# Handing out the input projection of a two-layer trunk in half pieces

## The chip, the cores and the metric

The kernel runs on 1 core of a Trainium2 chip. The metric is the device time of one execution in microseconds (us). Engine names are those of the profile: PE is TensorE's matmul, PEld its weight load, DVE is VectorE, ACT is ScalarE, POOL is GpSimd, SP is SyncE, which issues the DMAs. A "granted clock" of 1.00 is 2.4 GHz and 0.50 is 1.2 GHz; a figure between them is a mean over a stretch.

## What is computed

Two layers over 512 tokens (256 of context, 256 latent) of width 1024. A layer normalises, multiplies by one input projection, gives its columns to four mixers that scan the tokens in both directions, joins the four outputs, multiplies by an output projection and adds the result to the stream. Then comes a feed-forward block, dense in the first layer and a mixture of 8 experts in the second. Cut to the parts that matter here:

```python
def layer(x):
    h = modulated_rms_norm(x)
    p = h @ w_in                      # 28 tiles of 128 columns
    y = concat(rglru(p), rwkv7(p), mlstm(p), gdn(p))
    x = x + gate * (y @ w_out)
    return x + gate2 * ffn(modulated_rms_norm(x))
```

## The kernel before, in words

Every matrix is split in two parts of fp32r, a high and a low one, and a product is three matmuls: high by high, low activation by high weight, high activation by low weight (`mm3`). A weight tile comes by DMA (`wsplit`, L251, issued at L257), ACT casts the high part (`whi`, L258) and DVE subtracts for the low part (`wlo`, L259). In an order or a profile a matmul `pj<-hh,whi` or `pj<-hl,whi` or `pj<-hh,wlo` is one of those three: of the input projection first, of the output projection later.

The mixer stage of a layer is written by `mixers` (L1494). It is a loop that hands out work by turns. In a turn the projection gives one **piece**: `inproj` (L415) yields after the 12 matmuls of one k for the first four column tiles, and after 4 of the 8 k, 12 matmuls too, for the 24 other tiles. Then the **filling** may move (the modulation blocks of later work, `mod_block`, whose weights `mw` come from `mod_w`), and then each of three **lanes** may move by some steps. A lane is a queue of mixer units; a step is what a unit does up to its next `yield`. How far each may go in a turn is a credit, which grows by the numbers of the table `PACE`: three for the lanes, one for the filling, chosen by the count of turns `n`. After the last piece the turns go on until the lanes are empty.

When the projection is through and only one mixer is left, the **early sums** begin: `outproj_part` (L1692) sums the output projection over the finished mixers' rows, for one of 8 column tiles m at a time: 6 of the 8 k, 18 matmuls. It loads the old stream (`pst`, L1700), adds (`resid`, L1718) and writes the sum to DRAM (`xo`, L1703). The loop takes one of its nine steps in every turn (L1640). The last mixer is the mLSTM (`mlstm`, L1290): its end is a chain over DVE, ACT and PE (L1393 to L1424), and its output is split into `hh` and `hl` (L1286, L1287). Then `outproj` (L1706) loads the early sums back (`xT<-xo`, L2032) and adds the last 2 k of each column tile, 6 matmuls each, 48 in all: the **final sums**. The first layer works on 512 columns there, the second on the 256 latent ones.

What stands in each engine's queue is fixed when the program is built. It follows the order in which the code is written, with small shifts: a few matmuls of a piece may stand ahead of a lane's step and the others behind it.

Of the kernel before, what the change touches and what calls it, by code (L numbers as in the profile page):

```python
# [180 lines left out]
class Trunk:  # L181
# [233 lines left out]
    def inproj(self, l, tiles, evac, lat_only=()):  # L415
        if sorted(tiles[0:4]) == list(range(4)):
            pss = [self.pjt() for _ in range(2)] + [self.ps(), self.ps()]
            for k in range(8):
                wh, wl = self.wsplit(self.t["w_in0"][l, :, k], 4, P)
                for i in range(4):  # L420
                    tl, lo = tiles[i], 256 if i in lat_only else 0
                    self.mm3(pss[i][:, lo:512], wh[:, tl], wl[:, tl], self.hh[:, k, lo:512], self.hl[:, k, lo:512],
                             k == 0, k == 7)
                if k < 7:
                    yield
            for i in range(4):
                evac(i, pss[i])
            yield
        for i, tl in enumerate(tiles):
            if tl < 4:  # L430
                continue
            ps = self.pjt()
            lo = 256 if i in lat_only else 0
            for k in range(8):
                if k % 4 == 0:
                    wh, wl = self.wsplit(self.t["w_in"][l, tl - 4, :, k:k + 4], 4, P)
                self.mm3(ps[:, lo:512], wh[:, k % 4], wl[:, k % 4], self.hh[:, k, lo:512], self.hl[:, k, lo:512],
                         k == 0, k == 7)
                if k % self.PIECE[l] == self.PIECE[l] - 1 and k < 7:
                    yield  # L440
            evac(i, ps)
            yield
# [1051 lines left out]
    def mixers(self, l, xsrc, xdst):  # L1494
# [129 lines left out]
        while self.going or filling or any(self.lanes):  # L1624
            if self.going:
                self.ph(f"inp{l}")
                self.going = next(pr, "end") != "end"
            pace = next((p for e, p in self.PACE[l] if n < e), self.PACE[l][-1][1])
            n += 1
            credit[3] += pace[3]  # L1630
            while filling and credit[3] >= 1:
                self.ph(f"modx{l}")
                filling = next(md, "end") != "end"
                credit[3] -= 1
            if part is None and not self.going and len(self.fill[l]) < full - 1 and len(self.left) <= self.PART[l]:
                self.early = [k for i, m in enumerate(("lru", "rwkv", "gdn", "mlstm")) if m not in self.left for k in (2 * i, 2 * i + 1)]
                part = self.outproj_part(l, self.early, xsrc, xdst)
            if part is not None:
                self.ph(f"outp{l}")
                next(part, None)  # L1640
            for i, q in enumerate(self.lanes):
                credit[i] = min(credit[i], 0) if not q else credit[i] + pace[i]
                while credit[i] >= 1:
                    credit[i] -= 1
                    while q:
                        self.ph(self.lab.get(id(q[0]), "mix"))
                        r = next(q[0], "end")
                        if r != "end":
                            self.lab[id(q[0])] = r
                            break  # L1650
                        q.pop(0)
# [2 lines left out]
        return [k for k in range(8) if k not in self.early]  # L1654

    PART = [1, 1]
    PIECE = [4, 4]
    NPP = (3, 2, 2)
    LANE = dict(gates=1, rwkv=0, gdn=1, mlstm=2, lru=2)
    LATE = (0, 2)  # L1660
# [537 lines left out]
```

## Time and profile before

| what | value |
|---|---|
| median of 3 runs | 1906.63 us (1901.4 to 1910.62) |
| the profiled execution | 1907.89 us |
| its span, first to last instruction | 1906.1 us |
| PE busy | 1726.9 us (91%) |
| PEld busy | 1428.8 us (75%) |
| DVE busy | 1233.9 us (65%) |
| ACT busy | 1009.4 us (53%) |
| mean granted clock | 0.923 |

Durations below come from the profiled execution, so a sum is made against its 1907.89 us. It lies 1.3 us above the median. Busy time on PE overlaps itself: a matmul of 512 columns is shown as 0.39 us long while the next one starts 0.23 us later. So starts are compared, or a count is divided into a stretch.

### The profile page before, as it was taken

The numbers are of one execution on the slowest core, as the hardware profiler recorded it, in microseconds if no ns is written. First come the engines' busy times: TensorE is split into PE (matmuls) and PEld (weight loads), VectorE is DVE, ScalarE is ACT, GpSimd is POOL, SyncE is SP. The second block draws the span as 40 slices with busy tenths as digits, with TensorE's granted clock in tenths as the row PEclk, the third lists the DMA queues.
The fourth block names the chain that finished last, engine by engine and source line by source line (L and its number), as shares of the span: only waits on it lengthen the run. The fifth ranks groups of instructions, "written<-read, shape, count | busy, mean of one in ns | idle before, by whom it ended". The sixth has DMA issues, their size and how long they took to land. (4 is left out here: it accounts for less than half of the span.)

```text
span 1906.1 us, 34059 instructions
## 1 busy us (share of the span) xinstructions
PE 1726.9 (91%) x13291; PEld 1428.8 (75%) x13291; DVE 1233.9 (65%) x2527; ACT 1009.4 (53%) x1760; POOL 33.5 (2%) x88
## 2 busy tenths in 40 slices
PE   4989988997987999999979898998886999999996
PEld 2767666774765888888867665776775999999995
DVE  4577368777656433333366747797655888888886
ACT  4554465774534333332255453677435776777673
POOL 0000001000000000000000000000000000000000
PEclk8969898998998999999988898999687999999998
DMA  7433333244452333333334444411264998989891
GB/s 278 145 105 124 121 128 112 66 136 152 140 178 67 97 98 99 95 97 94 97 131 138 134 142 144 137 62 49 69 197 147 350 347 298 354 286 356 314 342 74
DMA packets 130921, 309.71 MB, mean 162 GB/s; under 512 B 14208, under 2 KB 40064, under 8 KB 130624
## 3 DMA queue, kind: packets, MB, share of 16 engines
q1 hardware_dynamic: 130752, 307.46, 47.8%
q8 instruction: 106, 1.74, 0.4%
q14 instruction: 63, 0.52, 0.1%
HBM read 286.76 MB, written 20.64 MB: 161 GB/s over the span
## 5 line engine op out<-in xcount | busy, mean ns | idle before, releaser
L259 DVE TENSOR_TENSOR wlo<-w,whi 128x512 fp32r<-128x512 f32 (+2 forms) x488 | 501.0, 1033 | 327.0 <-ACT whi L258 311.6
L258 ACT CAST whi<-w 128x512 fp32r<-128x512 f32 (+2 forms) x488 | 436.7, 898 | 413.2 <-PE pj L244 145.4
L244 PE MATMUL pj<-hh,whi 128*128 128x512 f32 (+1 forms) x544 | 225.3, 415 | 32.1 <-ACT whi L258 15.7
L244 PE MATMUL pj<-hh,wlo 128*128 128x512 f32 (+1 forms) x544 | 220.7, 407 | 5.4 <-DVE wlo L259 5.2
L244 PE MATMUL pj<-hl,whi 128*128 128x512 f32 (+1 forms) x544 | 215.9, 397 | 0.4 <-DVE hl L1287 0.2
L244 PE MATMUL pm<-whi,xgh 128*128 128x384 f32 (+1 forms) x512 | 168.2, 329 | 0.0
L244 PE MATMUL pm<-whi,xgl 128*128 128x384 f32 (+1 forms) x512 | 166.6, 325 | 0.0
L244 PE MATMUL pm<-wlo,xgh 128*128 128x384 f32 (+1 forms) x512 | 166.1, 324 | 0.0
L244 PEld LDWEIGHTS pj<-hh,whi 128*128 128x128 f32 x544 | 114.1, 210 | 61.2 <-ACT whi L258 20.8
L244 PE MATMUL pj<-mw,sc 128*32 128x256 f32 x768 | 107.0, 433 | 53.1 <-DMA mw<-in_mod_w 52.9
L244 PEld LDWEIGHTS pj<-hh,wlo 128*128 128x128 f32 x544 | 113.2, 208 | 35.1 <-DVE wlo L259 11.2
L244 PEld LDWEIGHTS pj<-hl,whi 128*128 128x128 f32 x544 | 114.1, 210 | 17.7 <-DVE hl L1287 0.9
L244 PE MATMUL pd<-whi,hth 128*128 128x256 f32 x352 | 100.1, 285 | 0.3
L244 PE MATMUL pd<-wlo,hth 128*128 128x256 f32 x352 | 99.2, 282 | 0.0
L244 PEld LDWEIGHTS pj<-mw,sc 128*32 128x32 f32 x768 | 27.4, 114 | 95.8 <-DMA mw<-in_mod_w 53.2
L244 PE MATMUL pd<-whi,htl 128*128 128x256 f32 x352 | 99.2, 284 | 0.0
L244 PEld LDWEIGHTS pm<-wlo,xgh 128*128 128x128 f32 x512 | 96.5, 188 | 0.0
L244 PEld LDWEIGHTS pm<-whi,xgh 128*128 128x128 f32 x512 | 96.4, 188 | 0.0
L244 PEld LDWEIGHTS pm<-whi,xgl 128*128 128x128 f32 x512 | 96.2, 188 | 0.0
L244 PE MATMUL pj<-fh,whi 128*128 128x512 f32 x176 | 68.6, 390 | 0.0
L244 PE MATMUL pj<-fh,wlo 128*128 128x512 f32 x176 | 68.5, 389 | 0.0
L244 PE MATMUL pj<-fl,whi 128*128 128x512 f32 x176 | 68.5, 389 | 0.0
(617 smaller groups left out, 3470.5 us busy)
## 6 DMA issues: line engine op xcount, KB each, us to landing
w<-in_moe_gu SPq DMA_DIRECT2D x96, 768.0 KB, 6.8
mw<-in_mod_w SPq DMA_DIRECT2D x160, 256.0 KB, 3.1
w<-in_w_in SPq DMA_DIRECT2D x112, 256.0 KB, 3.0
w<-in_moe_d SPq DMA_DIRECT2D x32, 768.0 KB, 6.1
w<-in_ffn_gu SPq DMA_DIRECT2D x88, 256.0 KB, 2.7
w<-in_moe_e SPq DMA_DIRECT2D x32, 640.0 KB, 5.5
w<-in_moe_gv SPq DMA_DIRECT2D x32, 512.0 KB, 4.5
pp<-pd SPq DMA_DIRECT2D x46, 256.0 KB, 3.7
```

What stands on the lines that cost most here:

```text
L244: self.nc.tensor.matmul(out, lhsT, rhs, start=start, stop=stop)
L258: nc.scalar.copy(hi, w)
L259: nc.vector.tensor_sub(lo, w, hi.bitcast(F32))
```

## The change

A piece becomes half as large: 6 matmuls, by a second `yield` among the first four tiles and by `PIECE` 2 in place of 4 for the others. The count of turns at which a row of `PACE` ends is doubled, and every pace is halved, so that lanes and filling move as far per matmul of the projection as before. The early sums' call of one step per turn is not touched by the diff.

```diff
@@ inproj
                              k == 0, k == 7)
+                    if i == 1:
+                        yield
                 if k < 7:
                     yield
@@ mixers
-            pace = next((p for e, p in self.PACE[l] if n < e), self.PACE[l][-1][1])
+            pace = next((p for e, p in self.PACE[l] if n < self.HALVES * e), self.PACE[l][-1][1])
+            pace = [p / self.HALVES for p in pace]
             n += 1
@@
-    PIECE = [4, 4]
+    PIECE = [2, 2]
+    HALVES = 2
```

How the queues move is shown at three places. The first is PE's queue in the first layer's projection, where the first small matmuls stand between its pieces (`pj_750` is the projection, `pc` are the small ones of the gates). One piece of the difference:

```order
 L244 MATMUL pj_750<-hl,whi_752 128x512
 L244 MATMUL pj_750<-hh,wlo_753 128x512
+L244 MATMUL pc_769<-smb_763,cst 64x256 x2
+L244 MATMUL pc_769<-sma_559,cst 64x256
 L244 MATMUL pj_750<-hh,whi_752 128x512
 L244 MATMUL pj_750<-hl,whi_752 128x512
```

A step that stood behind 12 projection matmuls now stands after 6 of them, and the other 6 follow it.

The second is PE's queue at the end of the first layer's mixers, in the program before. `drb` is read by the last state products of the last mLSTM unit, `cst,srd` are the four transposes near its end, and `pj_5750` is the eighth early sum:

```order
L244 MATMUL pm_5575<-sre_5256,drb_5305 128x66 x2
L244 MATMUL pj_5604<-hl,whi_5606 128x512
L244 MATMUL pj_5640<-hh,whi_5642 128x512
L244 MATMUL pj_5698<-hh,whi_5700 128x512
L1416 MATMUL pm_5738<-cst,srd_5307 128x128 x4
L244 MATMUL pj_5750<-hh,whi_5752 128x512
```

And in the changed program, where `pj_5684` is the eighth early sum and `pj_5800` the first final one:

```order
L244 MATMUL pj_5684<-hh,wlo_5705 128x512
L244 MATMUL pm_5719<-smask_351,identb 128x264
L244 MATMUL pm_5719<-drc_5095,dra_5667 128x66 x8
L244 MATMUL pm_5719<-sre_5256,drb_5337 128x66 x2
L1418 MATMUL pm_5774<-cst,srd_5339 128x128 x4
L244 MATMUL pj_5800<-hh,whi_5802 128x512
```

Before, 50 matmuls of early sums (one row of each sum is shown) stand between the last state products and the transposes, and 18 more behind the transposes. Now all of the early sums stand ahead of the state products, and nothing stands between these, the transposes and the first final sum.

The third is the same place in the second layer, in the program before (`dmb` is read by the last state products, `cst,smd` are the transposes, `pj_13596` is the first final sum):

```order
L244 MATMUL pm_13367<-ms_13134,dmb_13184 128x66 x2
L244 MATMUL pj_13396<-hl,whi_13416 128x256
L244 MATMUL pj_13453<-hh,whi_13455 128x256
L1416 MATMUL pm_13492<-cst,smd_13186 128x128 x4
L244 MATMUL pj_13596<-hh,whi_13598 128x256
```

And in the changed program (`pj_13473` is the eighth early sum, `rro,pick` opens the last step):

```order
L244 MATMUL pm_13455<-rro_9456,pick 128x256 x2
L244 MATMUL pj_13473<-hh,wlo_13494 128x256
L244 MATMUL pm_13507<-smask_8717,identb 128x264
L244 MATMUL pm_13507<-v_2276_13090,dma_13456 128x66 x8
L244 MATMUL pm_13507<-ms_13169,dmb_13254 128x66 x2
L1418 MATMUL pm_13562<-cst,smd_13256 128x128 x4
L244 MATMUL pj_13596<-hh,whi_13598 128x256
```

Before, 56 matmuls of early sums stand between the last state products and the transposes; now none does. Between the last `rro,pick` and the products with `dma` stood 17 of them, and now stand 7.

## Rows read from the trace of the kernel before

**Rows 1.** The page's head: the span and the count of instructions

```profile
span 1906.1 us, 34059 instructions
```

**Rows 2.** Busy time by stage: stretch, length, PE, PEld, DVE, ACT, POOL busy (count), clock, DMA

```profile
95.00:500.00 405.00, 364.31 (x3834) 266.06 (x3833) 279.78 (x754) 228.46 (x481) 14.53 (x37) 0.89 0.38 123
...
600.00:955.00 355.00, 353.40 (x1555) 291.77 (x1556) 130.10 (x205) 113.12 (x191) 0.00 (x0) 1.00 0.33 96
...
1024.00:1320.00 296.00, 269.45 (x3040) 200.85 (x3039) 209.10 (x574) 172.37 (x360) 13.19 (x32) 0.91 0.36 113
```

**Rows 3.** Waits of PE, 95 to 500 us: us in total, times, longest

```profile
PE pj L244 <- DMA mw<-in_mod_w: 22.9, 15, 3.2
```

**Rows 4.** Waits of PE, 1024 to 1320 us

```profile
PE pj L244 <- DMA mw<-in_mod_w: 11.0, 8, 3.1
```

**Rows 5.** What touches pj alone, by stretch: columns of rows 2, without POOL

```profile
542.90:555.80 12.90, 12.86 (x50) 10.18 (x50) 1.74 (x4) 0.00 (x0) 0.90 0.37 124
555.90:563.20 7.30, 7.13 (x30) 5.55 (x30) 1.65 (x4) 0.00 (x0) 1.00 0.53 176
568.60:580.80 12.20, 11.50 (x36) 7.77 (x36) 5.09 (x12) 0.00 (x0) 0.82 0.50 159
1399.70:1407.95 8.25, 7.77 (x56) 6.95 (x56) 1.44 (x3) 0.00 (x0) 1.00 0.49 150
1411.90:1428.80 16.90, 12.21 (x48) 10.56 (x48) 3.34 (x8) 0.00 (x0) 0.52 0.82 276
```

**Rows 6.** Timeline, first layer's last chain, PE and DVE: start, us, instruction [idle before]

```profile
542.01 0.89 PE L244 MATMUL pm<-sre,drb 64*128 64x66 f32 x4
...
542.94 0.17 DVE L1393 TENSOR_SCALAR dn<-pm 128x8 f32<-128x8 f32 x1 [3.19 <-PE pm L244]
...
544.50 0.42 DVE L1400 TENSOR_TENSOR srd<-srb 128x256 f32<-128x256 f32 x1
...
549.67 0.17 DVE L345 TENSOR_TENSOR rq<-rq 128x8 f32<-128x8 f32 x1
...
550.88 0.17 DVE L345 TENSOR_TENSOR rq<-rq 128x8 f32<-128x8 f32 x1
```

**Rows 7.** Timeline, second layer's last chain, PE, ACT and DVE

```profile
1399.13 0.61 PE L244 MATMUL pm<-ms,dmb 64*128 64x66 f32 x4
...
1403.23 0.63 ACT L1403 ACTIVATE sma<-smd 128x512 f32<-128x512 f32 x1 [0.59 <-DVE smd L1400]
...
1403.90 0.69 DVE L1405 TENSOR_REDUCE ss<-sma 128x8 f32<-128x512 f32 x1
...
1408.69 0.69 DVE L1407 TENSOR_TENSOR smd<-smd,rq 128x512 f32<-128x512 f32 x1
...
1409.53 0.63 PE L1416 MATMUL pm<-cst,smd 128*128 128x128 f32 x4 [1.62 <-DVE smd L1407]
...
1410.20 1.03 DVE L1424 TENSOR_TENSOR smc<-pm,smb 128x256 f32<-128x256 f32 x2
...
1411.26 0.62 ACT L1286 CAST hh<-smc 128x512 fp32r<-128x512 f32 x1 [2.85 <-DVE smc L1424]
...
1411.93 0.50 PE L244 MATMUL pj<-hh,whi 128*128 128x256 f32 x2 [1.77 <-ACT hh L1286]
```

**Rows 8.** Timeline, second layer, the step ahead of that chain

```profile
1393.33 1.16 ACT L1374 ACTIVATE dma<-pm,ctm 128x128 f32<-128x128 f32 x4
...
1394.52 1.23 DVE L1377 TENSOR_TENSOR dma<-dma,sma 128x1024 f32<-128x1024 f32 x1
...
1395.91 1.90 PE L244 MATMUL pm<-v,dma 128*128 128x66 f32 x16
```

**Rows 9.** Timeline, first layer, SP's issues of the reload and DVE's first sum

```profile
561.27 0.33 SPq L1703 DMA_DIRECT2D xo<-pst  x1
...
564.28 3.65 SPq L2032 DMA_DIRECT2D xT<-xo  x8
...
567.62 1.66 DVE L1718 SCALAR_TENSOR_TENSOR xT<-pj,mod,xT 128x256 f32<-128x256 f32 x4 [3.86 <-DMA xT<-xo]
```

## The prediction

> **What bounds the kernel now.** I read the span first [rows 1], then the table of busy time by stage [rows 2]. It shows where the change can act. In the dense feed-forward stretch (600 to 955 us) PE is busy for 353.4 of 355 us at a clock of 1.00, and the change is not there. Its places are the two stretches in which the projection is handed out beside the lanes: 95 to 500 us, where PE is idle for 405 - 364.3 = 40.7 us at a mean clock of 0.89, and 1024 to 1320 us, with 296 - 269.5 = 26.5 us idle at 0.91 [rows 2]. PE is the engine that sets the time there, with DVE busy for about 70% of both stretches.
>
> The table of waits says what the idle time is. The largest single item is the filling's weights, 22.9 us in the first stretch and 11.0 us in the second, in waits of up to 3.2 us [rows 3, 4]. The rest, 17.8 + 15.5 = 33.3 us, is spread over short waits for the lanes' DVE and ACT work and for the split of the projection's weights.
>
> Then comes the end of each layer's mixers, which the diff does not name and the order view does. There the reader is to see that before the change the early sums keep PE full while the last mLSTM unit runs its chain on DVE and ACT: 50 matmuls in 12.90 us of the first layer with PE busy for 12.86, and 56 in 8.25 us of the second [rows 5].
>
> **The change, part by part.** No work is added or removed: matmuls, DMAs and casts are the same in number, and the weights of the projection and of the filling follow each other in SP's queue in the same sequence. Only places in the queues move.
>
> *Projection stretches: a gain of 11 us taken, 0 to 22 as bounds.* A lane's step that stood behind 12 matmuls now has 6 on either side. Two dependent steps of one lane that stood next to each other get matmuls between them, and a wait for DVE or ACT is then covered by work. The 34 us of waits for the filling's weights I leave where they are: they end with a DMA, a block of the filling keeps its size, and the three buffers that these loads go round in are freed in the same turn. Of the other 33.3 us, nothing at all may go, since the order before already lets other steps in between the matmuls of a piece at many places; that is the lower bound. Two thirds, 22 us, is the upper one, since a step now meets the projection at twice as many places, but the longest chains of the lanes run where no projection is left. I take the third, 11 us: three lanes and the projection stand in the queue by turns, and a half piece lies beside a given wait about once in three.
>
> The clock is part of these stretches. A mean of 0.89 and 0.91 between the levels 1.0 and 0.5 means about 22% and 18% of the time at 1.2 GHz, 89 and 53 us, although the pieces are whole [rows 2]; in the dense stretch it is never there. I take the clock as unchanged in the sum. The Trainium skill (TensorE: Matmul & The Clock Gate, section Loop structure matters more than you think) has matmuls stay back to back, with other work beside them, and says that PE goes cold where it waits between them. By that rule, halving the bursts speaks against the change and the sum would come out slower, which is the third rival; the trace agrees only in that the clock stays up where matmuls are dense.
>
> *The end of the first layer's mixers: 6.1 us lost.* The early sums take one step in every turn, and a turn now moves the lanes half as far. So they are used up before the last unit's chain, and that chain runs with PE idle. Its length, without anything between: from the end of the state products at 542.90 us to the end of L1400, 2.0 us [rows 6]; L1403 on ACT 0.63; L1405 0.69; thirteen small steps of the root, at 0.20 us each (549.67 to 550.88 is six of them) 2.6; L1407 0.69; transposes 0.63; L1424 1.03; the cast to `hh` 0.62 [rows 6, 7]. That is 8.9 us, and with some 0.5 us for seven hand-overs, 9.4 us. (Before, the same chain took 12.2 us in the second layer, from 1399.74 to 1411.93, because the sums' casts and adds stood between its steps [rows 7].) After it, 12 final matmuls can run, and the others need the early sums back. These were issued 3.0 us after the last write and the first sum began 3.3 us after that, at 567.62 [rows 9]; this put 5.5 us of idle time on PE before. Now the write is long done, but the new tile takes the place of the lane's buffers, so I let its load start when the lane ends: `hl` comes 0.7 after `hh`, issue 0.1, landing 3.3, two sums 1.0, together 5.1 us after `hh`. The last 36 matmuls take 12.2 us [rows 5]. The 68 early matmuls that stood in this stretch are paid earlier at what they cost now: 12.9 us for 50, and 18 times 7.3/30, 4.4 us [rows 5]. New: 17.3 + 9.4 + 5.1 + 12.2 = 44.0 us. Before: 542.90 to 580.8, 37.9 us. The difference is 6.1 us.
>
> *The end of the second layer's mixers: 5.4 us lost.* From the last state product to the first final matmul it was 12.2 us [rows 7]. Now it is 9.4 us of chain, and the 56 early matmuls are paid ahead of it with their 8.25 us [rows 5]: 17.6 us. What follows from `hh` on is unchanged.
>
> *The step ahead of these chains: 1.6 us lost.* Four exponentials (1.16 us) and a product (1.23 us) lie between the last `rro,pick` and the matmuls that read `dma` [rows 8]. In the second layer 17 early matmuls covered these 2.5 us; now 7 do, some 1.2 us with the mask, so 1.3 us opens. In the first layer 8 remain, of twice the columns, and 0.3 us opens.
>
> *Sum.* 6.1 + 5.4 + 1.6 - 11 = +2 us on 1907.89 us. That execution lies 1.3 us over the median shown, and I forecast **1909 us** for the median. No change that a measurement of this kernel could tell (0.5%, 9.5 us) is the likeliest. With gains of 4 to 22 us this case by itself gives 1898 to 1916.
>
> **The rivals.**
>
> *The gain isn't there: slower.* The queues in the projection stretches were interleaved finely already, so that half pieces change little where PE waits; in this sense the change does not do what it says, and only the two ends remain. For it speaks that half of the idle time there, 34 of 67 us, is the filling's DMA waits [rows 3, 4], which the change doesn't touch; against it, that steps really did move ahead of half a piece. Price: +13 us, about 1920 us. If the idle time brings the clock down, the first layer's 36 final matmuls go from 12.2 us to about 15.5 us (0.43 us each, twice the 0.215 of full speed, as the second layer's run at 0.52 [rows 5]), and it is 1923. It decides as soon as the gain is under 3.6 us.
>
> *The waits fall by half and the clock follows: faster.* With 16 us less of waits and two points more of mean clock over 701 us, 14 us, less the ends' 13, it is 17 us faster, about 1890 us. For it speaks that 33 us of waits, and the 142 us at 1.2 GHz that go with all of them, lie just where steps and pieces now alternate twice as often; against it, that the filling's waits, the longest ones, stay.
>
> *Shorter bursts let the clock fall: slower.* If the mean clock drops by three points over the 701 us, that is 21 us, and with the ends' 13 and half of the gain still there, 28 us: about 1935 us. That is the rule of the page named above. Against it speaks that the small matmuls between the pieces keep PE busy too.
>
> **How the numbers follow.** I give my forecast 0.48, the rival without the gain 0.27, the faster one 0.18 and the one with the clock 0.07. The range reaches from 1892, which leaves out about half of the faster case (0.09), to 1929, which takes in the rival without the gain and leaves out the clock's (0.07). Faster by over 0.5% is 0.18, within 0.5% 0.48, slower 0.34.
>
> **What would show it.** At both ends of the mixers PE should stand idle for about 9 us between the last state products and the first final sum, but for the four transposes, and the first layer's wait of 5.6 us for the early sums' return should be down to about 2 us. Between 95 and 500 us, and in the second layer's stretch, PE's waits other than for `mw` should add up to some 22 us and no longer to 33, with the waits for `mw` near 34 us and the clock within a point of 0.89 and 0.91. I am wrong if the ends are as short as before, which would mean that the chain was not what PE waited for, or if the waits for `mw` move by more than 8 us, which I left out of the sum.

## The result, and the profile after

The changed kernel takes 1922.59 us (median of 7 runs, 1916.86 to 1929.42), beside 1906.63 us before (7 runs on the same chip, 1896.14 to 1923.42). The ratio is 1.0075, with a 95% interval of 1.0046 to 1.0104: slower by 0.75%, some 14 us. The forecast was 1909 us and no change that can be told; the time lies in the range, and it is the one that the first rival gives, "the gain isn't there" (1920 to 1923).

The profiled execution of the changed kernel took 1918.79 us. Its page's head and the engines' shares, to set beside [rows 1] and the table of before:

```profile
span 1917.0 us, 34068 instructions
...
PE 1728.0 (90%) x13291; PEld 1420.8 (74%) x13291; DVE 1236.9 (65%) x2527; ACT 1009.8 (53%) x1760; POOL 33.6 (2%) x88
```

PE has the same work (1728.0 us, before 1726.9). To see where 10.9 us of span came from, I set the same DVE and ACT instructions of the two traces side by side and read by how much each starts later (median in a stretch). It is -7.7 us at 300 to 350 us of before's time, +9.7 at 500 to 520, +16.1 from 563 to 600, the same at 960, +17.0 at 1005 to 1020, +0.7 at 1362 to 1370, and +10.6 at the end. So there are four pieces: the first layer's projection stretch **+10**, its end **+6**, the second layer's stretch **-16**, its end **+10**. The change gained only in the second layer.

*The two ends.* In the first layer PE now does nothing between the last state products and the first final sum but the four transposes. The timeline of PE in the changed kernel there:

```profile
566.80 1.06 PE L244 MATMUL pm<-sre,drb 64*128 64x66 f32 x4
574.69 1.09 PE L1418 MATMUL pm<-cst,srd 128*128 128x128 f32 x4 [6.83 <-DVE srd L1409]
577.55 1.22 PE L244 MATMUL pj<-hh,whi 128*128 128x512 f32 x2 [1.77 <-ACT hh L1288]
```

From 567.86 (566.80 + 1.06) to 577.55 is 9.69 us, where before 50 early matmuls filled 12.90 us [rows 5]. The second layer's end:

```profile
1404.69 0.39 PE L244 MATMUL pm<-smask,identb 128*128 128x264 bf16 x2 [0.31 <-ACT dma L1376]
1406.98 2.00 PE L244 MATMUL pm<-v,dma 128*128 128x66 f32 x16 [1.90 <-DVE dma L1379]
...
1411.09 1.06 PE L244 MATMUL pm<-ms,dmb 64*128 64x66 f32 x4
1418.91 1.09 PE L1418 MATMUL pm<-cst,smd 128*128 128x128 f32 x4 [6.77 <-DVE smd L1409]
1421.84 0.79 PE L244 MATMUL pj<-hh,whi 128*128 128x256 f32 x2 [1.84 <-ACT hh L1288]
```

Again 9.69 us (1412.15 to 1421.84). The step ahead opens 0.31 + 1.90 us. Behind it PE is slow: the same four state products take 1.06 us here and 0.61 before [rows 7], the four transposes 1.09 and 0.63 [rows 7].

*The two stretches.* Busy time by stage, to set beside [rows 2] (stretch, length, PE, PEld, DVE, ACT, POOL busy with counts, clock, DMA):

```profile
95.00:500.00 405.00, 363.31 (x3720) 259.24 (x3721) 277.23 (x742) 222.18 (x465) 14.57 (x37) 0.89 0.38 119
1024.00:1320.00 296.00, 273.91 (x3099) 204.07 (x3097) 217.26 (x598) 180.06 (x374) 13.20 (x32) 0.95 0.39 123
```

PE's waits between 95 and 500 us in the changed kernel (us in all, times, longest), to set beside [rows 3]:

```profile
PE pj L244 <- DMA mw<-in_mod_w: 14.5, 12, 2.7
PE pj L244 <- ACT whi L258: 8.8, 4, 3.4
PE pj L244 <- DVE wlo L259: 4.5, 5, 1.8
```

The waits for the filling's weights fell from 22.9 to 14.5 us, which I had left out of the sum. Those for the projection's own weights rose: `whi` and `wlo` were 4.4 and 2.3 us before, with none over 1.2 us, and are 8.8 and 4.5 now, with two of about 3.3 us. In the second layer the wait for `mw` is as before [rows 4]:

```profile
PE pj L244 <- DMA mw<-in_mod_w: 10.5, 10, 2.9
```

Fixed windows hold different work in the two kernels, so I cut the second layer's stretch at the same instructions. Before:

```profile
1026.00:1365.00 339.00, 304.51 (x3467) 229.75 (x3464) 240.45 (x646) 189.96 (x395) 13.30 (x33) 0.88 0.34 107
```

And changed:

```profile
1043.00:1366.00 323.00, 291.81 (x3477) 218.17 (x3477) 239.39 (x648) 191.60 (x397) 13.32 (x33) 0.92 0.35 112
```

It is the same work in 16 us less. Idle time fell by only 34.5 - 31.2 = 3.3 us. The clock did the rest: a mean of 0.88 over 339 us is 81 us at 1.2 GHz, one of 0.92 over 323 us is 52 us.

Not all of the 16 us belongs to the change, for these are single executions. The kernel e3 below has whole pieces in the second layer, and its queues stand there in the order of before's; it takes 5 us less for the same work:

```profile
1046.00:1380.00 334.00, 300.14 (x3474) 227.22 (x3471) 240.68 (x647) 190.58 (x396) 13.33 (x33) 0.90 0.33 109
```

Aligned from 1005 to 1370 us, the profiles with whole pieces there (before, e3, e4, e10) stand at 0, -5, -5 and -6 us, those with half pieces (the change, e1, e2, e9) at -16, -15, -14 and -18. So some 12 us are left for the half pieces.

### The profile page after: what moved, and what is told of

It is laid out like the page before. It is cut to its first block, busy times and chain, and to the rows that moved or that the text cites. A ratio compares the mean times of both kernels' runs of the same rounds, so it can differ in the third digit from the quotient of the medians.

```text
span 1917.0 us, 34068 instructions
## 1 busy us (share of the span) xinstructions
PE 1728.0 (90%) x13291; PEld 1420.8 (74%) x13291; DVE 1236.9 (65%) x2527; ACT 1009.8 (53%) x1760; POOL 33.6 (2%) x88
## 5 line engine op out<-in xcount | busy, mean ns | idle before, releaser
L244 PE MATMUL pj<-hh,whi 128*128 128x512 f32 (+1 forms) x544 | 228.8, 422 | 32.3 <-ACT whi L258 17.8
```

What stands on the lines that cost most here:

```text
L244: self.nc.tensor.matmul(out, lhsT, rhs, start=start, stop=stop)
```

## What held the first layer up

The largest part of the first layer's loss sits in one place: aligned, the change falls back from -7.7 us at 320 to 340 us to +3.0 at 400 to 420. Another 6.7 us follow up to 500 us, which e9 and e10 below lose too (5.2 and 6.5 us); e2 and e4, with whole pieces, lose nothing there. The cause was not traced. Cut at the same work again, the stretch from 335 to 395 us of before:

```profile
335.00:395.00 60.00, 56.88 (x743) 43.23 (x738) 43.40 (x110) 40.62 (x81) 2.27 (x6) 0.97 0.29 90
```

In the changed kernel:

```profile
328.00:394.00 66.00, 59.19 (x753) 44.80 (x749) 45.44 (x112) 36.77 (x73) 2.27 (x6) 0.92 0.31 97
```

The timeline of the changed kernel around its middle shows why, SP's queue first:

```profile
348.91 0.33 SPq L1558 DMA_DIRECT2D pd<-pst  x1
349.32 0.88 SPq L257 DMA_DIRECT2D w<-in_w_in  x2
```

Then ACT:

```profile
348.22 0.66 ACT L1587 ACTIVATE pst<-pj 128x256 f32<-128x256 f32 x2
349.15 0.36 ACT L961 COPY srb<-pm 32x256 f32<-32x256 f32 x1 [0.27 <-PE pm L244]
353.47 1.29 ACT L258 CAST whi<-w 128x512 fp32r<-128x512 f32 x2 [3.95 <-DMA w<-in_w_in]
```

And PE:

```profile
350.21 0.56 PE L244 MATMUL pc<-rst,drc 64*64 64x64 f32 x12
354.14 0.50 PE L244 MATMUL pj<-hh,whi 128*128 128x512 f32 x1 [3.36 <-ACT whi L258]
```

Read upwards: PE waits 3.36 us for `whi`; ACT could not cast it, because the weight DMA landed late; that DMA was issued late, because it stands behind `pd<-pst` in SP's queue, the write of the tile finished before; and this write waited for ACT's evacuation, 348.22 to 348.88. The next tile's first matmuls come one turn after the evacuation in both kernels (`inproj` yields behind it), and a turn is now half as long. With whole pieces the first load stands ahead of the write (SP's queue in the kernel e2 below, whole pieces in this layer):

```profile
344.31 0.38 SPq L257 DMA_DIRECT2D w<-in_w_in  x1
345.33 0.33 SPq L1558 DMA_DIRECT2D pd<-pst  x1
345.75 0.38 SPq L257 DMA_DIRECT2D w<-in_w_in  x1
```

The experiments first tell the layers and the ends apart (e1 to e4), then test this wait (e5 to e12). Each time below stands with its ratio to runs of the kernel before from the same chip and the same series (medians 1905.28 us for e1 to e4, 1905.15 for e5 to e8, 1903.38 for e9 to e12), with its 95% interval in brackets.

## The layers and the ends apart

**e1: the change, with early sums one step every second turn.** Theory A is the prediction's account of the ends.

```diff
-                next(part, None)
+                if n % self.HALVES == 0:
+                    next(part, None)
```

> The change, with the early sums taken one step in every second turn, so that they move with the lanes as before. Theory A (the ends of the two layers cost what the change lost, because the early sums ran out ahead of the last chain): 13 to 17 us less than the change, 1904 to 1909 us, and PE's idle time between the last state products and the first final sum falls from 8.6 us to under 4 us in both layers. Theory B (the loss lies in the projection stretches, and the ends only show it): over 1917 us.

Measured: 1906.70 us (1887.19 to 1929.54, 12 runs), ratio 0.9997 [0.9968, 1.0026]. The whole 0.75% is gone when the early sums last to the end again, as theory A has it, and PE's idle time between the last state products and the first final sum falls to 2.1 us in the first layer and 3.4 in the second. In both projection stretches e1's queues stand in the order of the change's (two pairs of neighbours on PE apart), so this prices the ends alone. The runs scatter over 42 us.

**e2: half pieces in the second layer alone**, **e3: in the first alone.** Early sums move with the lanes in both. The rest of the diff, which makes each layer read its own number, is left out here.

```diff
-    PIECE = [2, 2]
-    HALVES = 2
+    PIECE = [4, 2]        # e3: [2, 4]
+    HALVES = (1, 2)       # e3: (2, 1)
```

> Whole pieces in the first layer, half pieces in the second, the early sums moving with the lanes in both. Theory A (half pieces gain about 14 us in the second layer's projection and lose about 9 in the first's): the first layer ends within 2 us of where it ended before the change, and the whole takes 1889 to 1897 us. Theory B (the gain seen in the second layer is chance of how it was entered, and is not tied to the pieces): 1902 to 1911 us.

> Half pieces in the first layer, whole ones in the second, the early sums moving with the lanes in both. Theory A: the first layer's projection loses about 9 us and nothing gains in the second: 1911 to 1919 us. Theory B: 1902 to 1909 us.

Measured: e2 1896.88 us, ratio 0.9960 [0.9937, 0.9982]; e3 1919.81 us, ratio 1.0077 [1.0053, 1.0101]. Half pieces are worth a gain in the second layer (8 us) and a loss in the first (15 us), with the ends covered in both; e2 lies in theory A's range and e3 0.8 us above it. The two add up to 1.0037, where e1, which has both, measured 0.9997; that gap isn't explained.

Theory A's other sign failed: e2's first layer ended 8.6 us earlier than that of before, and not within 2 us, although both have one order. Up to 500 us before, e2 and e4 share the order of their queues (a few neighbours on PE apart), and aligned there they stand at 0, -9.1 and -8.2 us; the change, e1 and e3 share theirs, and stand at +9.7, +9.5 and +20.0. So executions of one order differ by some 10 us in this stretch, the profile of before took long for its order, and the first layer lost more than the 10 us read above.

In e3 the 3.36 us wait is there again, and the clock behind it is worse than in the changed kernel's profile. Two windows of e3:

```profile
345.00:365.00 20.00, 16.64 (x122) 13.48 (x122) 9.80 (x15) 6.85 (x14) 0.00 (x0) 0.64 0.27 93
365.00:385.00 20.00, 20.00 (x244) 15.18 (x241) 8.06 (x27) 7.50 (x16) 1.05 (x2) 0.59 0.10 29
```

From 365 to 385 us PE waits for nothing and still runs at 0.59: the granted clock fell with the wait and was back only 30.7 us later. In e3 the work of before's 335 to 395 us takes 79 us (in e1 73):

```profile
325.00:404.00 79.00, 71.85 (x761) 55.37 (x751) 45.81 (x114) 37.29 (x75) 2.27 (x6) 0.74 0.25 81
```

**e4: the kernel before, with two early steps a turn**, so that the sums run out before the last chains with whole pieces too.

```diff
-                next(part, None)
+                next(part, None)
+                next(part, None)
```

> The kernel before with whole pieces, and the early sums taken two steps in every turn: the ends of the change alone. Theory A: 13 to 17 us more than before, 1919 to 1924 us, with 8 to 9 us of idle time of PE in each last chain. Theory B (the ends cost nothing by themselves): 1902 to 1911 us.

Measured: 1909.51 us, ratio 1.0035 [1.0015, 1.0055]. That is a miss: the ends cost 4 us by the medians and 7 by the ratio there, and not 13. In its profile PE idles for 8.6 us in each last chain (6.8 + 1.8), as theory A has it, and aligned the two ends lose 3.7 and 7.1 us. Taking the sums two at a time also moves them to another place among the lanes, so I priced the ends once more in e12.

## The write ahead of the weights

**e5: half pieces in the first layer alone, weights ahead of the write; e6: the kernel before with the same; e7: half pieces in both layers, early sums every second turn, with the same; e8: half pieces in the second layer alone, with the same.** From here on, theories A, B and C are about the first layer's loss, as the expectations state them. `wload` is the part of `wsplit` that issues the DMA. The part of the diff that all four share is in `inproj`:

```diff
+        ahead = None
...
                 if k % 4 == 0:
-                    wh, wl = self.wsplit(self.t["w_in"][l, tl - 4, :, k:k + 4], 4, P)
+                    wh, wl = self.wsplit(self.t["w_in"][l, tl - 4, :, k:k + 4], 4, P, w=ahead)
+                    ahead = None
...
+            if i + 1 < len(tiles):
+                ahead = self.wload(self.t["w_in"][l, tiles[i + 1] - 4, :, 0:4], 4, P)
             evac(i, ps)
```

> Half pieces in the first layer alone, early sums every second turn there as before, and one thing more, in both layers: the weights of a tile's first four k are issued on SP's queue before the finished tile's evacuation is written, so that the write of pst to pd no longer stands ahead of them. Theory A (what the first layer's half pieces lose comes from that write: PE waits 3.36 us for pj<-hh,whi near 351 us, and the clock is at half behind it): that wait falls under 1 us, the half-clock time of 95 to 500 us falls from 116 us (first layer alone in halves) to 78 to 92, and the time stands within 0.3% of the whole-piece kernel with the same early weights (its ratio to before is 0.998 to 1.006 if that kernel's is 1.000). Theory B (short pieces themselves cost the first layer its clock or time, wherever the write stands): the ratio stays at 1.005 to 1.010 and is 0.5% or more above that kernel's.

> The kernel before, whole pieces, with the weights of a tile's first four k issued ahead of the write of the finished tile, as control. In the whole-piece runs the load that matters near 345 us stands ahead of the write already, so theory A and theory B both expect 0.996 to 1.004 to before; a gain of over 0.5% would say that the write delays weights in whole pieces too.

> Half pieces in both layers, early sums one step every second turn, and the weights ahead of the write. Theory A: both layers are then at their best, the first as with whole pieces, the second with the gain of half pieces: 1893 to 1899 us (ratio 0.993 to 0.997), near the kernel with half pieces in the second layer alone (1896.9). Theory B: as without the early weights, 1904 to 1909 us (ratio 0.998 to 1.002).

> Half pieces in the second layer alone, early sums with the lanes, and the weights ahead of the write in both layers. Theory A and theory B: 0.993 to 0.998 to before, as without the early weights (0.996); theory A says the kernel with half pieces in both layers stands within 0.3% of it, theory B that that one is 0.5% slower.

Measured:

| kernel | us | ratio, 95% interval |
|---|---|---|
| e5, halves in the first layer | 1888.23 | 0.9907 [0.9876, 0.9938] |
| e6, whole pieces | 1912.23 | 1.0049 [1.0025, 1.0074] |
| e7, halves in both | 1884.24 | 0.9905 [0.9878, 0.9931] |
| e8, halves in the second layer | 1909.52 | 1.0023 [1.0001, 1.0044] |

Theory B falls: half pieces in the first layer do not cost it its time by themselves, they go from 1.0077 (e3) to 0.9907 (e5) when one load per tile is issued earlier, in both layers. In e5 no wait of PE for `whi` is left between 95 and 500 us, and the time at half clock there falls from e3's 116 us to 76. Theory A's numbers are not met either, for the effect is larger than the wait it names: e5 is 1.4% faster than its control e6, where A expected a tie, and e7 beats its 1893 to 1899 by 9 us. The controls are misses as well: with whole pieces in the first layer the same edit costs 0.5% (e6) and 0.6% (e8 against e2). The edit moves the order at every tile, so it is a blunt test.

**e9: the change, with the weights ahead of the write at one tile only; e10: e3 with the same.** The tile is the one of the 3.36 us wait. Up to the early sums, the queues keep their order but for some 40 us: from 346 to 386 us of the changed kernel, PE's queue in e9 holds another matmul at 205 of 420 places, and DVE's, ACT's and SP's queues change places there too.

```diff
-            if i + 1 < len(tiles):
+            if l == 0 and tiles[i + 1:i + 2] == [18]:
```

> The change, with one load issued earlier: the weights of the first four k of the projection's tile 18 in the first layer (the third mlstm tile) now stand ahead of the write of the tile finished before; every other tile as in the change. Theory A (that one write ahead of the weights, with the 3.36 us wait of PE and the half-speed clock behind it, is what the first layer's stretch lost): PE's wait for pj<-hh,whi near 354 us falls under 1 us, the half-clock time between 335 and 395 us falls from 10.2 us to 0 to 4, and the time falls by 7 to 14 us to 1908 to 1916 (ratio to before 1.000 to 1.005). Theory C (the first layer's loss is spread over the stretch, and it was the early weights of all tiles together that mended it): 1918 to 1927 (ratio 1.006 to 1.010), as the change.

> Half pieces in the first layer alone, early sums every second turn there, and the one load of tile 18 ahead of the write. Theory A: 0.998 to 1.003 to before (1901 to 1911), down from 1919.8 (1.0077), half-clock time of 335 to 395 us from 41 us to 0 to 10. Theory C: 1.005 to 1.009, as without it; the kernel with all loads early had 0.991.

Measured: e9 1907.43 us, ratio 1.0015 [0.9988, 1.0041], from 1.0075 [1.0046, 1.0104] for the change; e10 1906.29 us, ratio 1.0008 [0.9979, 1.0038], from 1.0077 [1.0053, 1.0101] for e3. In both pairs one load of 256 KB, issued ahead of a write, gives back 0.6 to 0.7%, some 12 us, and the intervals do not meet. Theory A has this (e9 came out 0.6 us under its range, and in it by the ratio). PE's wait for `whi` in this place is gone in both. What is left between 330 and 360 us is at most 1.1 us, for the evacuation itself (one row, the same in e9 and e10):

```profile
PE pj L244 <- ACT pst L1596: 1.1, 1, 1.1
```

SP's queue in e10:

```profile
343.16 0.33 SPq L1567 DMA_DIRECT2D pd<-pst  x1
343.58 0.38 SPq L305 DMA_DIRECT2D mw<-in_mod_w  x1
344.05 0.41 SPq L253 DMA_DIRECT2D w<-in_w_in  x1
```

One `w` is left behind the write, where the changed kernel had two; the other is issued at 323 us already, with the loads of the tile before. The work of before's 335 to 395 us now takes, in e10:

```profile
323.00:390.00 67.00, 62.55 (x757) 47.36 (x753) 46.07 (x114) 36.59 (x74) 2.27 (x6) 0.87 0.29 96
```

That is 12 us less than e3's 79. In e9 it is 63 us beside the 66 of the change, and the rest of the 13 us by which its profiled first layer is shorter lies mostly ahead of the edit, where the queues are the same; one execution's clock differs from another's by that much. By the means of one order it is 73 us (the change, e1, e3: 66, 73, 79) against 65 (e9, e10), so some 8 us of the 12 lie in this place, and it still takes 6 us more than with whole pieces (60, 58 and 58 in before, e2 and e4). So the run times carry the verdict that this load matters. Whether it acts by the wait alone, or also by the new order of the 40 us behind it, no run here tells. The expected half-clock time was too low for both (at most 4 and 10 us, measured 6.8 and 17.1).

**e11: e7, with this one load put back behind the write.**

```diff
-            if i + 1 < len(tiles):
+            if i + 1 < len(tiles) and not (l == 0 and tiles[i + 1] == 18):
```

> The fastest kernel so far (half pieces in both layers, early sums every second turn, weights ahead of the write: 1884.2, ratio 0.9905), with the one load of tile 18 in the first layer put back behind the write. Theory A: the wait of some 2 to 4 us for pj<-hh,whi comes back near 340 us and costs 5 to 20 us in all: 1890 to 1905 (ratio 0.993 to 1.000). Theory C: 1883 to 1888 (0.989 to 0.992), no different.

Measured: 1891.38 us (1871.33 to 1894.82, 6 runs), ratio 0.9893 [0.9847, 0.9939]. Inconclusive: the median is 7 us above e7's, as A would have it, but the ratios are the same, as C would. In the profile (an execution of 1893.90 us) the wait is back, with 1.58 us:

```profile
343.88 0.80 PE L244 MATMUL pj<-hh,whi 128*128 128x512 f32 x1 [1.58 <-ACT whi L263]
```

The granted clock is at half from 343.6 us on, for 30.7 us. Another run of the same kernel took 1871.33 us, the fastest of all that were made; it left no trace. The queues are the same in it, so the place seems to make the loss possible, not certain.

**e12: the change, with early sums every turn, and the weights ahead of the write at every tile.** Against e7 it differs by the early sums' pace alone.

> The change (early sums every turn, so that they run out at both layers' ends) with the weights of every tile ahead of the write. Against the same kernel with early sums every second turn (1884.2, runs of 1882.6 to 1888.3) it prices the two ends alone. The prediction's price is 11.5 us (6.1 and 5.4): 1894 to 1898 (ratio 0.995 to 0.998). By the whole-piece kernel with two early steps a turn it is 6 to 7 us: 1890 to 1892 (0.993 to 0.995).

Measured: 1900.68 us, ratio 0.9970 [0.9944, 0.9995]. Beside e7's 0.9905 that is 0.65%, 12 us by the ratios and 16 by the medians. The ends' price of 11.5 us stands (the ratio lies in its range, the median 2.7 us above it); e4's smaller price does not hold where the pieces are halves.

## Why the prediction was right or wrong

*The ends: right, with some luck in the terms.* The chain of 9.4 us measured 9.69 in both layers. The first layer's 6.1 us came out as 6 in the aligned traces. But what follows the cast to `hh` took 20.3 us (577.50 to 597.80) and not 17.3, with the clock at half until 583.4 us and 2.9 us of waits for `wlo`; so what stands ahead of the chain cost some 3 us less than I took. The wait of 5.6 us for the early sums' return is down to 0.3, and the longest wait among the last 36 matmuls is now one of 1.6 us for `wlo`. The second layer's end, with the step ahead of it, was to lose 5.4 + 1.3 us and lost 10. Of the missing 3 us, 0.9 are the step ahead, which opened 2.2 us and not 1.3, and 1.2 the clock: PE waited 1.90 us for `dma`, and from 1409.4 us on, 2.4 us after that wait, it ran at half speed. The four groups of state products took 3.24 us (1408.91 to 1412.15) where they took 2.00 before (1397.74 to 1399.74), and the transposes 1.09 for 0.63. I had carried durations over from a stretch that PE kept busy into one in which it stands idle. e1 against the change (0.78%) and e12 against e7 (0.65%) price both ends together at 12 to 16 us, where the sum had 13.1.

*The gain in the projection stretches: the step that failed.* I took 11 us for both stretches together, as a third of PE's short waits, with the clock unchanged. The waits other than for `mw` did not fall from 33 us to 22. In the fixed windows they are 405 - 363.3 - 14.5 = 27.2 us and 296 - 273.9 - 10.5 = 11.6 us, 39 in all, 17.8 and 15.5 before. The waits for `mw` fell by 8.9 us, which is past the 8 us that the prediction gave as its own limit. In the profiles the second layer gained 16 us, most of it by the clock, and the first lost 10; by the runs of e2 and e3 it is a gain of 8 and a loss of 15. e1, which has the half pieces without the ends' cost, measures this step as a whole: 0.9997 [0.9968, 1.0026], no gain, where 11 us would be 0.9942. The range held because it reached down to no gain; that the two layers cancelled is luck.

*What failed inside this step.* I wrote that the weights of the projection and of the filling "follow each other in SP's queue in the same sequence". They do, among themselves, but not against the writes of finished tiles. A piece of half the size halves the time between a tile's evacuation and the next tile's first matmul, and the load stood behind the write that waits for that evacuation. e9 and e10 bear this out as far as they go: one such load, issued earlier, gave back 12 us, with a new order behind it. I had looked for what a step ahead of a matmul gains and not for what a load behind a store loses.

*The rivals.* "The gain isn't there" gave the right time, and its reason was half right: only the ends' price remained, but because one layer's gain met the other's loss. "The waits fall by half and the clock follows" is half of what the second layer did: the clock rose (0.88 before and 0.90 in e3, 0.92 in the change), but the idle time fell by 3.3 us of 34.5 and not by half. "Shorter bursts let the clock fall" is what the first layer looked like, yet e5 shows that short pieces alone are not the reason: with the loads earlier they run at a clock of 0.91 between 95 and 500 us. The rule of the Trainium skill (TensorE: Matmul & The Clock Gate, section Loop structure matters more than you think), that PE goes cold where it waits between matmuls, agrees with e3, where the clock is at 0.64 and 0.59 in the two windows shown, with the 3.36 us wait at their start. The wait is not the whole of it: behind the same wait in the changed kernel the clock was at half for 3.4 us, and e10, without a wait for `whi`, has 17.1 us at half clock in this stretch.

*What stays open.* Why issuing all loads early helps half pieces by a further 1% (e5 against e10) and costs whole pieces 0.5% (e6) isn't settled; nor is the loss between 400 and 500 us that the half pieces have in e9 and e10 too. One thing seen is that a second wait for `whi`, of 3.29 us and ending at 276 us in the changed kernel, is still in e9 and e10 (3.42 and 2.35 us) and not in e5 and e7; it was not tried by itself.

The lowest median is that of e7, half pieces with early sums every second turn and the weights ahead of the write: 1884.24 us, by the ratios 1% faster than before and 1.7% faster than the change, with its six runs within 6 us. By their ratios, e5 (0.9907) and e11 (0.9893) can't be told from it.

## What to carry to other kernels

When work is handed out in smaller pieces per turn, everything else that moves once a turn moves too: look for each call that is not scaled, and for what it was covering at the far end of the program. Then look at each DMA queue for a load that stands behind a store, and ask how long before its use the store's producer ends; halving the piece halves that time. And cost a piece of idle time on PE with what follows it at half clock, not by the wait alone. Before you read a few microseconds between two profiles as the change's, set two executions of one order side by side: here they lay up to 10 us apart in one stretch.

## What the hardware showed that I had not expected

The clock's answer to one wait varies widely, and not only between different programs: the changed kernel, e1 and e3 have one order in their queues up to 500 us. At PE's wait for `whi` in this place the half-clock spell was 3.4 us in the changed kernel (wait 3.36 us), 17.1 in e1 (1.87), 30.7 in e3 (3.36), and in e11, whose order is another, 30.7 (1.58). So the wait's length does not tell the loss: one of 1.6 us was followed by as long a spell at 1.2 GHz as one of 3.4 us. In e3 PE was busy for 20.00 of 20 us from 365 us on, with 244 matmuls, and the clock stayed at 0.59 on the mean.
